# TensorE's loop without a lead-in and with its head placed by `head_slot`, and joined copies of neighbouring ranges, in a float32 transpose of 8192 x 8192

## Chip, cores, metric

One core of one Trainium2 chip. The metric is the device time of a whole execution, in microseconds (us). A transfer has "landed" when the last raise of its semaphore is in the trace; the "granted clock" is the share of TensorE's full clock that the trace records.

## The reference

```python
def setup_inputs():
    return {"x": np.random.randn(8192, 8192).astype(np.float32)}

def reference(x):
    return np.transpose(x)
```

268.44 MB go in and as many come out. Nothing is computed.

## The kernel before

The input is worked through in T = 128 tiles of 128 rows x 4096 columns (two slabs of columns, 64 tiles each). For each tile: a load of 2 MiB into one of three input buffers; 32 transposes of 128 x 128 on TensorE into the eight PSUM banks, four to a bank; eight copies to SBUF, by ScalarE (even banks) and VectorE (odd banks). The copies fill eight "windows" of output, one for each bank, each eight tiles wide; the windows are staggered, so that in each tile one of them is full and is stored (2 MiB as a rule). There are nine window buffers for eight open windows. All loads but the first three and all stores are issued from ScalarE's queue.

```python
        ins = [nc.alloc_sbuf_tensor(f"in{k}", [P, J], dt).ap() for k in range(NIN)]            # NIN = 3
        regs = [nc.alloc_sbuf_tensor(f"reg{k}", [P, B * W * P], dt).ap() for k in range(NREG)]  # NREG = 9
        pss = [nc.alloc_psum_tensor(f"ps{k}", [P, B * P], dt).ap() for k in range(NR)]          # NR = 8
        ...
        def transposes(t):
            k = t % NIN
            nc.tensor.sem_inc(s_ld[k], -16).wait_op(s_ld[k], 16, "sem-ge")
            for q in range(NR):
                if t:
                    nc.tensor.sem_inc(s_bank[q], -1).wait_op(s_bank[q], 1, "sem-ge")
                for b in range(B):                                                              # B = 4
                    tr = nc.tensor.transpose(pss[q][:, b * P:(b + 1) * P],
                        ins[k][:, q * B * P + b:(q + 1) * B * P - B + b + 1:B], ident)
                    if b == B - 1:
                        tr.then_inc(s_pe, 1)
        ...
        for t in range(T % NIN):                        # lead-in: two tiles
            transposes(t)
        with nc.Fori(0, T // NIN, engines=[nc.tensor.engine]):   # 42 turns of three tiles
            for t in range(NIN):
                transposes(T % NIN + t)
        ...
        for t, (s, c) in enumerate(chunks):
            closing = []
            for q in range(NR):
                e = q % 2
                eng = (nc.scalar, nc.vector)[e]
                ...                                     # a new window waits for its buffer's store
                eng.wait_ge(s_pe, t * NR + q + 1)
                ...                                     # one copy of 128 x 512
                before = []
                if e == 0:
                    before, closing = closing, []
                ...                                     # full windows go to closing, the bank is freed
                for k in before:
                    store(*k)
            for k in closing:
                store(*k)
            if t + NIN < T:
                nc.scalar.wait_ge(s_pe, (t + 1) * NR)
                load(t + NIN)
```

## Time and profile before

| | before |
|---|---|
| time, first three runs | 1264.88 us (1264.87 to 1265.91) |
| DMA engines | share 1.01 and 428 GB/s from 2 to 1254 us |
| TensorE (matmul) | busy 744.9 us, 59%; granted clock 0.745 |
| VectorE, ScalarE | busy 348.1 and 294.1 us, 28 and 23% |

The groups of instructions of the kernel before, by line (line, engine, operation, out<-in, forms, count, then busy us, mean ns of one, and idle time before them with what ended it):

```profile
L112 PE MATMUL ps<-ident,in 128*128 128x128 f32 x4096 | 744.9, 364 | 489.8 <-PEq L110 481.4
L189 DVE COPY reg<-ps 128x512 f32<-128x512 f32 x512 | 348.1, 690 | 887.2 <-PE ps L112 733.5
L187 ACT COPY reg<-ps 128x512 f32<-128x512 f32 x512 | 292.9, 588 | 941.5 <-PE ps L112 746.2
```

All three engines are idle for hundreds of us, waiting for each other or for transfers. The busy shares say who is not the bound.

### The profile page before, as it was taken

What the parts mean: (1) busy time and instruction counts of PE and PEld (TensorE: products, weight loads), DVE (VectorE), ACT (ScalarE), POOL (GpSimd) and SP (SyncE); (2) the same over time, 40 slices, a digit from 0 to 9 for tenths busy, and PEclk for the clock granted to TensorE, in tenths of its full rate; (3) what the DMA queues carried; (4) which work ended last, traced back from release to release, by engine and by line L of the source; (5) the groups of instructions that cost most, each with busy time, mean ns of one, the idle gap of its engine ahead of it and who ended that gap; (6) DMA issues with size and microseconds to landing.
All of it is one profiled execution on the core that took longest, in us unless ns stands there. A gap on an engine that the chain in (4) does not pass through costs nothing. (4 is left out here: it accounts for less than half of the span.)

```text
span 1261.5 us, 11043 instructions
## 1 busy us (share of the span) xinstructions
PE 744.9 (59%) x4096; PEld 724.6 (57%) x4096; DVE 348.1 (28%) x512; ACT 294.1 (23%) x513; POOL 0.7 (0%) x6
## 2 busy tenths in 40 slices
PE   5656656565566656565655565656566665656561
PEld 5656656565566656565655555656455655655561
DVE  3322322223222322232222232232222322222220
ACT  3322222222222222222222222222222222222220
POOL 0000000000000000000000000000000000000000
PEclk9877776768677777778687778686867777686765
DMA  9999999999999999999999999999999999999998
GB/s 381 426 427 429 425 430 431 428 429 431 429 429 431 429 429 430 429 430 431 426 428 411 429 429 429 430 431 429 429 431 428 430 430 429 429 429 430 430 429 355
DMA packets 39277, 537.00 MB, mean 426 GB/s; under 512 B 4320, under 2 KB 4832, under 8 KB 6240
## 3 DMA queue, kind: packets, MB, share of 16 engines
q10 hardware_dynamic: 38832, 530.60, 98.9%
q1 hardware_dynamic: 432, 6.29, 1.2%
q14 instruction: 12, 0.10, 0.0%
q8 instruction: 1, 0.02, 0.0%
HBM read 268.44 MB, written 268.44 MB: 426 GB/s over the span
## 5 line engine op out<-in xcount | busy, mean ns | idle before, releaser
L112 PE MATMUL ps<-ident,in 128*128 128x128 f32 x4096 | 744.9, 364 | 489.8 <-PEq L110 481.4
L112 PEld LDWEIGHTS ps<-ident,in 128*128 128x128 f32 x4096 | 724.6, 219 | 509.9 <-issue 509.9
L189 DVE COPY reg<-ps 128x512 f32<-128x512 f32 x512 | 348.1, 690 | 887.2 <-PE ps L112 733.5
L187 ACT COPY reg<-ps 128x512 f32<-128x512 f32 x512 | 292.9, 588 | 941.5 <-PE ps L112 746.2
L187 ACT ACT_TABLE_LOAD x1 | 1.3, 1283 | 0.9 <-SPq L68 0.9
L84 POOL TENSOR_SCALAR_AFFINE_SELECT ident<-ident 128x128 f32<-128x128 f32 x1 | 0.3, 294 | 0.2 <-POOL ident L82 0.2
L82 POOL MEMSET ident<- 128x128 f32 x1 | 0.2, 205 | 0.5 <-SPq L68 0.5
L224 POOL MEMSET const-bfloat16-1.0<- 128x1 bf16 x1 | 0.1, 102 | 0.0
L224 POOL MEMSET const-uint8-127<- 128x1 uint8 x1 | 0.1, 102 | 0.0
L224 POOL MEMSET const-float32-0.0<- 128x1 f32 x1 | 0.1, 99 | 0.2 <-issue 0.2
L224 POOL MEMSET const-float32-1.0<- 128x1 f32 x1 | 0.1, 99 | 0.0
## 6 DMA issues: line engine op xcount, KB each, us to landing
in<-in_x_dram ACTq DMA_DIRECT2D x125, 2048.0 KB, 22.8
out_dram<-reg ACTq DMA_DIRECT2D x114, 2048.0 KB, 19.4
out_dram<-reg ACTq DMA_DIRECT2D x4, 1792.0 KB, 17.6
in<-in_x_dram SPq DMA_DIRECT2D x3, 2048.0 KB, 11.7
out_dram<-reg ACTq DMA_DIRECT2D x4, 1536.0 KB, 15.1
out_dram<-reg ACTq DMA_DIRECT2D x4, 1280.0 KB, 16.3
out_dram<-reg ACTq DMA_DIRECT2D x4, 1024.0 KB, 16.6
out_dram<-reg ACTq DMA_DIRECT2D x4, 768.0 KB, 16.3
```

The costliest lines, as they stand in the source:

```text
L82: nc.gpsimd.memset(ident, 0.0).then_inc(s_id, 1)
L84: nc.gpsimd.affine_select(out=ident, in_=ident, compare_op=mybir.AluOpType.not_equal, fill=1.0, base=0, pattern=[[-1, P]], channel_multipl ...
L112: tr = nc.tensor.transpose(pss[q][:, b * P:(b + 1) * P], ins[k][:, q * B * P + b:(q + 1) * B * P - B + b + 1:B], ident,)
L187: cp = nc.scalar.copy(out=o, in_=i)
L189: cp = nc.vector.tensor_copy(out=o, in_=i)
L224: nc = _bacc.Bacc("TRN2", target_bir_lowering=False, num_devices=1)
```

## The change

Its intent is less work beside the transfers: half as many bank waits on TensorE, 631 copies instead of 1024, and a loop whose head `head_slot=0` puts at a set place in TensorE's program. (The recorded texts call that place a block boundary, and I say "the boundary" below; experiment 2 takes it away.) The eight banks become four double banks, and one copy moves both halves if their two places in SBUF have the same stride. The nine window buffers become one tensor, so that one access pattern can reach two of them.

```diff
-        regs = [nc.alloc_sbuf_tensor(f"reg{k}", [P, B * W * P], dt).ap() for k in range(NREG)]
-        pss = [nc.alloc_psum_tensor(f"ps{k}", [P, B * P], dt).ap() for k in range(NR)]
+        SIZE = B * W * P
+        regs = nc.alloc_sbuf_tensor("regs", [P, NREG * SIZE], dt).ap()
+        pss = [nc.alloc_psum_tensor(f"ps{k}", [P, 2 * B * P], dt).ap() for k in range(NR // 2)]
...
-            for q in range(NR):
-                if t:
-                    nc.tensor.sem_inc(s_bank[q], -1).wait_op(s_bank[q], 1, "sem-ge")
-                for b in range(B):
+            for h in range(NR // 2):
+                nc.tensor.sem_inc(s_bank[h], -1).wait_op(s_bank[h], 1, "sem-ge")
+                for b in range(2 * B):
...
-        for t in range(T % NIN):
-            transposes(t)
-        with nc.Fori(0, T // NIN, engines=[nc.tensor.engine]):
-            for t in range(NIN):
-                transposes(T % NIN + t)
+        for h in range(NR // 2):
+            nc.tensor.sem_inc(s_bank[h], 1)
+        with nc.Fori(0, T // NIN + 1, engines=pe, head_slot={pe[0]: 0}) as turn:
+            with nc.tensor.If(turn > 0):
+                transposes(NIN - 1)
+            nc.tensor.wait_ge(s_id, 2)
+            for k in range(NIN - 1):
+                transposes(k)
...
-            for q in range(NR):
-                e = q % 2
+            for h in range(NR // 2):
+                e = h % 2
...
+                gap = place[1][0] - place[0][0]
+                runs = [(0, 1)]
+                if place[0][1] != place[1][1] or abs(gap) >= 2 ** 15:
+                    runs = [(0,), (1,)]
+                eng.wait_ge(s_pe, t * NR // 2 + h + 1)
...
+                for u in runs:
+                    off, dist = place[u[0]]
+                    dims = [list(regs.ap[0]), [gap, len(u)], [dist, B], [1, P]]
+                    o = bass.AP(regs.tensor, regs.offset + off, dims)
...
+                    cp = nc.scalar.copy(out=o, in_=i) if e == 0 else nc.vector.tensor_copy(out=o, in_=i)
```

The stores and loads, their sizes and their order are untouched.

More of the change, by code (lines that the diff above doesn't have):

```diff
@@ L77 @@
         s_st = [nc.alloc_semaphore(f"s_st{k}") for k in range(NREG)]
-        s_bank = [nc.alloc_semaphore(f"s_bank{q}") for q in range(NR)]
+        s_bank = [nc.alloc_semaphore(f"s_bank{q}") for q in range(NR // 2)]
         s_pe = nc.alloc_semaphore("s_pe")
@@ L100, in load, with transposes @@
             ).then_inc(s_ld[t % NIN], 16)
-        def transposes(t):
-            k = t % NIN
+        def transposes(k):
             nc.tensor.sem_inc(s_ld[k], -16).wait_op(s_ld[k], 16, "sem-ge")
-            for q in range(NR):
-                if t:
-                    nc.tensor.sem_inc(s_bank[q], -1).wait_op(s_bank[q], 1, "sem-ge")
-                for b in range(B):
+            for h in range(NR // 2):
+                nc.tensor.sem_inc(s_bank[h], -1).wait_op(s_bank[h], 1, "sem-ge")
+                for b in range(2 * B):
+                    j = (2 * h + b // B) * B * P + b % B
                     tr = nc.tensor.transpose(
-                        pss[q][:, b * P:(b + 1) * P],
-                        ins[k][:, q * B * P + b:(q + 1) * B * P - B + b + 1:B],
+                        pss[h][:, b * P:(b + 1) * P],
+                        ins[k][:, j:j + B * P - B + 1:B],
                         ident,
                     )
-                    if b == B - 1:
-                        tr.then_inc(s_pe, 1)
+                tr.then_inc(s_pe, 1)
         T = len(chunks)
-        nc.tensor.wait_ge(s_id, 2)
-        for t in range(T % NIN):
-            transposes(t)
-        with nc.Fori(0, T // NIN, engines=[nc.tensor.engine]):
-            for t in range(NIN):
-                transposes(T % NIN + t)
+        assert T % NIN == NIN - 1
+        pe = [nc.tensor.engine]
+        for h in range(NR // 2):
[6 more added lines that the diff above has]
+                transposes(k)
         for t in range(NIN):
@@ L144, in store @@
                 dst = dst.rearrange("(q b) i -> q b i", q=P)
-                src = regs[r][:, base:base + B * rows]
+                src = regs[:, r * SIZE + base:r * SIZE + base + B * rows]
                 base += B * rows
@@ L162 @@
             closing = []
-            for q in range(NR):
-                e = q % 2
+            for h in range(NR // 2):
+                e = h % 2
                 eng = (nc.scalar, nc.vector)[e]
-                if q not in window:
-                    span = (q - c) % W + 1
-                    r = free.pop(0)
-                    parts = [(s, c, min(c + span, CH))]
-                    if c + span > CH and t + span < T:
-                        parts.append((s + 1, 0, c + span - CH))
-                    window[q] = (t, r, parts)
-                    if stored[r]:
-                        eng.wait_ge(s_st[r], 16 * stored[r])
-                t0, r, parts = window[q]
-                k = [p[0] for p in parts].index(s)
-                base = B * P * sum(z - a for _, a, z in parts[:k])
-                _, a, z = parts[k]
-                view = regs[r][:, base:base + B * (z - a) * P].rearrange("p (b i) -> p b i", b=B)
-                o = view[:, :, (c - a) * P:(c - a + 1) * P]
-                i = pss[q].rearrange("p (b i) -> p b i", b=B)
-                eng.wait_ge(s_pe, t * NR + q + 1)
-                if e == 0:
-                    cp = nc.scalar.copy(out=o, in_=i)
-                else:
-                    cp = nc.vector.tensor_copy(out=o, in_=i)
@@ new lines @@
+                place = []
+                for q in (2 * h, 2 * h + 1):
+                    if q not in window:
+                        span = (q - c) % W + 1
+                        r = free.pop(0)
+                        parts = [(s, c, min(c + span, CH))]
+                        if c + span > CH and t + span < T:
+                            parts.append((s + 1, 0, c + span - CH))
+                        window[q] = (t, r, parts)
+                        if stored[r]:
+                            eng.wait_ge(s_st[r], 16 * stored[r])
+                    t0, r, parts = window[q]
+                    k = [p[0] for p in parts].index(s)
+                    base = r * SIZE + B * P * sum(z - a for _, a, z in parts[:k])
+                    _, a, z = parts[k]
+                    place.append((base + (c - a) * P, (z - a) * P))
@@ L190 @@
+                ends = [q for q in (2 * h, 2 * h + 1) if closes(window[q], t)]
+                gap = place[1][0] - place[0][0]
[3 more added lines that the diff above has]
+                eng.wait_ge(s_pe, t * NR // 2 + h + 1)
                 before = []
@@ L192 @@
                     before, closing = closing, []
-                if closes(window[q], t):
-                    cp.then_inc(s_cp[e], 1)
-                    copied[e] += 1
-                    closing.append((q, e, copied[e]))
-                    eng.wait_ge(s_cp[e], copied[e])
-                    eng.sem_inc(s_bank[q], 1)
-                else:
-                    cp.then_inc(s_bank[q], 1)
+                for u in runs:
+                    off, dist = place[u[0]]
+                    dims = [list(regs.ap[0]), [gap, len(u)], [dist, B], [1, P]]
+                    o = bass.AP(regs.tensor, regs.offset + off, dims)
+                    i = pss[h][:, u[0] * B * P:(u[-1] + 1) * B * P]
+                    i = i.rearrange("p (l b i) -> p l b i", b=B, i=P)
+                    cp = nc.scalar.copy(out=o, in_=i) if e == 0 else nc.vector.tensor_copy(out=o, in_=i)
+                    mine = [q for q in ends if q - 2 * h in u]
+                    if mine:
+                        cp.then_inc(s_cp[e], 1)
+                        copied[e] += 1
+                        closing += [(q, e, copied[e]) for q in mine]
+                    if u is runs[-1]:
+                        if mine:
+                            eng.wait_ge(s_cp[e], copied[e])
+                            eng.sem_inc(s_bank[h], 1)
+                        else:
+                            cp.then_inc(s_bank[h], 1)
                 for k in before:
@@ L205 @@
             if t + NIN < T:
-                nc.scalar.wait_ge(s_pe, (t + 1) * NR)
+                nc.scalar.wait_ge(s_pe, (t + 1) * NR // 2)
                 load(t + NIN)
```

## The prediction

> **What bounds the kernel now.** I read the page first, its slices and its DMA part, because a transpose computes nothing: it moves 268.44 MB in and as much out.
>
> ```profile
> PE   5656656565566656565655565656566665656561
> DVE  3322322223222322232222232232222322222220
> ACT  3322222222222222222222222222222222222220
> DMA  9999999999999999999999999999999999999998
> GB/s 381 426 427 429 425 430 431 428 429 431 429 429 431 429 429 430 429 430 431 426 428 411 429 429 429 430 431 429 429 431 428 430 430 429 429 429 430 430 429 355
> HBM read 268.44 MB, written 268.44 MB: 426 GB/s over the span
> ```
>
> TensorE is busy in five to six tenths of every slice, the two copying engines in two to three, and the 16 DMA engines in nine or more of all but the last. The rate is flat at 429 GB/s or so. So the DMA engines are the bound, and everything that the change touches (TensorE's program, the copies) runs beside them.
>
> Next I asked for stretches, to see how much of the span is not at the full rate:
>
> ```profile
> 2.00:1254.00 1252.00, 744.88 (x4096) 724.56 (x4096) 348.15 (x512) 293.04 (x513) 0.00 (x0) 0.75 1.01 428
> 0.00:2.00 2.00, 0.00 (x0) 0.00 (x0) 0.00 (x0) 1.10 (x1) 0.70 (x6) 1.00 0.18 33
> 1254.00:1262.00 8.00, 0.00 (x0) 0.00 (x0) 0.00 (x0) 0.00 (x0) 0.00 (x0) 0.50 0.34 143
> ```
>
> The last two columns are the DMA share and the GB/s. For 1252 us the share is 1.01 at 428 GB/s. Only the first 2 us and the last 8 us are below, and they moved 33 x 2 us = 0.07 MB and 143 x 8 us = 1.14 MB, which at 428 GB/s would have taken 2.8 us. So at most 10 - 2.8 = 7.2 us of 1261.5, 0.6%, are not at the DMA's rate[...]. No change to the compute engines can take more than this away.
>
> The chain that ended last is no guide here: it names 1% of work, the last tile's, since a queued DMA is not a step of it. The waits tell who waits for whom:
>
> ```profile
> ACT reg L187 <- PE ps L112: 746.2, 384, 7.3
> DVE reg L189 <- PE ps L112: 733.5, 400, 10.4
> PE ps L112 <- PEq L110: 481.4, 125, 5.1
> ACT reg L187 <- DMA out_dram<-reg: 192.5, 45, 9.1
> DVE reg L189 <- DMA out_dram<-reg: 153.3, 39, 8.3
> ```
>
> The 125 waits of TensorE are one per tile (128 tiles). They are put down to the bank wait of L110, but the timeline shows the 32 transposes of one tile back to back (6.06 to 6.44 us when the granted clock is low) and then an idle stretch of about 3.5 us until the next tile. So I take the real releaser to be the load of the tile, which the DMA delivers every 1253 / 128 = 9.8 us. TensorE has about 3.5 us to spare in each.
>
> Last, how far ahead the transfers are issued:
>
> ```profile
> in<-in_x_dram ACTq DMA_DIRECT2D x125, 2048.0 KB, 22.8
> out_dram<-reg ACTq DMA_DIRECT2D x114, 2048.0 KB, 19.4
> ```
>
> A 2 MiB transfer takes 2.097 / 428 = 4.9 us of all engines. A load lands 22.8 us after its issue, a store 19.4. This adds up: three input buffers turn over in 3 x 9.8 = 29.4 us, and 22.8 of queue plus the 6.4 us that TensorE reads is 29.2. So at each issue about three other transfers, 14.7 us of work, lie ahead in the queue. An issue that comes 1 to 3 us later shortens this queue and nothing else.
>
> [...] The trace does not show the loop paying for it now: its compare-and-branch took 208 ns, the next matmul followed at once, and the fetch queue moved 12 packets, 0.10 MB[...]. [...]
>
> **The change, part by part.** The instruction order of both kernels shows that all 266 transfers of ScalarE's queue are the same, in the same sequence; the three first loads too. Bytes, descriptor sizes and order do not change. This is the main reason for the number.
>
> 1. Copies. ScalarE: 512 become 192 joined and 128 single (where the two places have different strides). VectorE: 201 joined and 110 single. [...] ScalarE's busy time: 128 x 0.588 + 192 x 1.015 = 270 us, from 293. VectorE's: 110 x 0.69 + 201 x 1.223 = 322 us, from 348. Some 25 us less on each, all of it beside the DMA: 0 us on the path.
>
> 2. Semaphores of TensorE. 8 bank waits per tile become 4: 1016 waits of 51 ns become 512, about 26 us of sequencer time, 0.2 us a tile, inside the 3.5 us of idle time. 0 us.
>
> 3. The loop. One lead-in of two tiles goes; a conditional part and one more turn come: 43 turns with a second branch of about 0.2 us, 9 us in all, in the same idle time. At the start TensorE waits until 8.4 us for its first load, so an extra fetch there is hidden. 0 us.
>
> 4. What becomes later. A copy now waits for eight transposes instead of four, 0.5 to 0.85 us, and takes 0.4 to 0.5 us longer, so stores are issued 1 to 2 us later; loads not, as they wait for the whole tile. In the middle the 14.7 us of queue absorbs it. I therefore expect the store's time from issue to landing to fall from 19.4 to about 18, and the landing itself to stay.
>
> 5. The tail is the one place without a queue to hide in. No loads follow there. The last load landed at about 1228.2 us; behind it lay two stores[...]. Before, the first of the eight last stores was issued at 1231.8. After, it comes behind both copies of the third pair: the sixth group of transposes is done at 1233.6, two single copies take 1.2 us, so it is issued at 1234.9, 3.1 us later, and its data begin about 1 us after, at 1236. That is just in time; I put 0 to 2 us on it, 0.5 in the middle.
>
> Sum: 1264.9 + 0.5, less a few tenths if something at the start gains: 1265.2 us.
>
> **Rivals.** A: the gain intended. If fetches or copies were on the path, 25 us of copies and 26 us of waits would come off, 2% each. Against it: the DMA share of 1.01 for 1252 us. Only the 7.2 us of the ends are open, so even in the best case about 1258 us. B: the coarser hand-over starves the DMA. Twice as large a unit in PSUM means four places instead of eight, and one copy that waits for a store to free its place now holds up two groups. The waits for stores (84 times, 346 us) speak for it. Against it: when such a store lands, three transfers are still queued, and what must follow (two copies of 1.0 us and an issue of 0.6 us) takes 3 us of those 14.7. If I am wrong and 1 us were lost in each tile, the time would be 1390 us; 0.2 us a tile makes 1290. C: the branch at every turn, or the conditional part, makes TensorE wait for a fetch. [...] but a turn has 3 x 3.5 us to spare; the time stays 1265. D: the tail empties the queue by more than I allow: 1267 to 1268.
>
> **Range and chances.** The three timed runs lie within 1.04 us. Nothing in the stretch of 1252 us should move; the ends can move by about -2 to +3 us. Eight times in ten: 1262.5 to 1268. Faster by over 2% would need less than 1239.6 us, below the 1254 us in which the bytes pass at 428 GB/s: 0.5%. Slower by over 2% needs 0.2 us of starvation in every tile or a surprise in the new branches: 1.5%.
>
> **What would show it.** Right: DMA share at 1.01 in the middle and the slices at 428 to 431 GB/s; VectorE near 322 us and ScalarE near 270 in 311 and 320 copies; a joined copy near 1.02 and 1.22 us; the store's time to landing shorter, at 18 us or so; the last stores first issued at about 1235, perhaps with a dip in the DMA share around 1236. Wrong: slices in the middle under 425 GB/s, or TensorE waits longer than the 3.5 to 5 us of now with DMA share under 1, would mean B or C. A span shorter by more than 7 us would mean that the DMA rate is not the limit I take it for.

The forecast was 1264.9 + 0.5 us, less a few tenths, 1265.2 us; parts 1 to 4 stood in it as 0 us each, the tail as 0.5, and terms from which parts 1 and 5 were worked out are among the cuts. What they leave open:

- That no rate was left to win was not shown; the slices of the kernel before read 425 to 431 GB/s in the middle but for one of 411.
- In "paying for it", "it" is a fetch of instructions at each turn. The "fetch queue" is the profile's instruction queue q14, with its 12 packets in 42 turns.
- The 1.015 and 1.223 us of a joined copy, and the 270 and 322 us made of them, were my estimates. The page of the changed kernel has 1013 and 1224 ns, which is 425 and 534 ns more than the 588 and 690 ns of a single copy before, and 262.9 and 316.0 us.
- "Just in time" speaks of the moment at which the queue was to run dry, put at about 1236 us with an allowance that no trace shows. In the kernel before, the last packet ended at 1259.80 us and the last landing came at 1260.20, 0.4 us later. The 1 us from an issue to its data is in that trace: the first load was issued at 0.94 us and its first packet of 16 KiB began at 1.94.

## The result

The changed kernel took 1265.55 us (median of six runs, 1263.88 to 1266.72), the kernel before 1265.35 us in the same comparison (six runs, 1264.87 to 1265.91). The ratio is 1.0001, 95% interval 0.9988 to 1.0014. Ratios here are the mean time of one kernel's runs over that of the other's of the same rounds, so not quite the ratio of the medians that I quote. Differences under about 1.6 us (0.0013 of the time, the half width of the interval) are not resolved. The outputs are right.

The slices and the DMA part of the page of the changed kernel:

```profile
PE   5665565565556555665556655656556655656561
DVE  2322222222222222223222222222222222222220
ACT  2312121122212211222212121122212121122120
DMA  9999999999999999999999999999999999999998
GB/s 367 430 426 426 426 428 430 429 431 430 429 428 430 430 430 428 430 429 429 430 421 420 428 429 427 427 426 428 427 431 429 431 429 429 429 430 429 430 429 364
```

And the stretch from 2 to 1254 us (the last three columns: granted clock, DMA share, GB/s):

```profile
2.00:1254.00 1252.00, 747.47 (x4096) 726.98 (x4096) 316.03 (x311) 261.83 (x321) 0.00 (x0) 0.75 1.01 427
```

The rate is the same 426 to 431 GB/s as before in all but a few slices: the first, the last, and two (421 and 420; before, one of 411) in the middle, where one slab of columns ends and stores are cut in two. The groups of copies, with forms kept apart, and the DMA issues (count, KB each, median us from issue to landing):

```profile
L208 DVE COPY regs<-ps 128x1024 f32<-128x1024 f32 x201 | 245.4, 1224 | 700.5 <-PE ps L114 537.4 <-DMA out_dram<-regs 161.9
L208 ACT COPY regs<-ps 128x1024 f32<-128x1024 f32 x192 | 193.5, 1013 | 746.7 <-PE ps L114 519.2 <-DMA out_dram<-regs 225.8 <-ACT regs L208 0.5
L208 DVE COPY regs<-ps 128x512 f32<-128x512 f32 x110 | 70.8, 686 | 221.3 <-PE ps L114 170.2 <-DMA out_dram<-regs 50.8
L208 ACT COPY regs<-ps 128x512 f32<-128x512 f32 x128 | 68.7, 589 | 225.7 <-PE ps L114 174.4 <-DMA out_dram<-regs 51.0
```

```profile
in<-in_x_dram ACTq DMA_DIRECT2D x125, 2048.0 KB, 22.5
out_dram<-regs ACTq DMA_DIRECT2D x114, 2048.0 KB, 18.3
```

The engines do less, as intended: VectorE 316.0 us and ScalarE 262.9 us, 32 and 31 us under before. The stores reach the queue later and keep their place among the loads: they land 18.3 us after issue instead of 19.4. (In this one profile loads and stores alike land about 1.4 us later than before; experiments 2 and 4 come back to that.) The last stores, in the timeline of the changed kernel and in stretches of 2 us (the last two columns are the DMA share and GB/s):

```profile
1236.36 15.47 ACTq L28 DMA_DIRECT2D out_dram<-regs  x8
```

```profile
1234.00:1236.00 2.00, 2.00 (x12) 2.00 (x11) 0.75 (x2) 0.83 (x2) 0.00 (x0) 0.55 0.85 360
1236.00:1238.00 2.00, 0.42 (x4) 0.23 (x2) 1.29 (x2) 0.24 (x1) 0.00 (x0) 1.00 0.45 187
1238.00:1240.00 2.00, 0.00 (x0) 0.00 (x0) 0.00 (x0) 0.00 (x0) 0.00 (x0) 0.81 1.10 454
```

Here is the predicted dip: a share of 0.45 for 2 us, 1.1 us of all engines. Before, the same stretch reads:

```profile
1236.00:1238.00 2.00, 0.00 (x0) 0.00 (x0) 0.00 (x0) 0.50 (x1) 0.00 (x0) 0.79 1.01 427
```

And one thing that I had not foreseen: the first matmul. Timelines of the start, before and then after:

```profile
8.40 9.34 PE L112 MATMUL ps<-ident,in 128*128 128x128 f32 x64 [8.40 <-PEq L107]
```

```profile
9.92 9.61 PE L114 MATMUL ps<-ident,in 128*128 128x128 f32 x64 [9.92 <-PEq L111]
```

TensorE starts 1.5 us later. So two small losses are to be seen, 1.5 us at the start and 1.1 us at the end, and neither shows in the time. The experiments are about where they went.

**A reading that the page does not give.** Each load's semaphore is raised 16 times, and the trace has the time of each. I call each raise the landing of a share, and take it for that of one of the 16 DMA engines; this is my reading and was not shown, as the trace does not name the engine. "The slowest engine" below is a name for the last of the 16 raises. What the trace does show is how far the 16 shares are apart, by rank. In the kernel before, all 16 shares of the first load landed within 0.46 us of each other (7.80 to 8.26 us). From about 150 us on the last came 3.5 us behind the first, from the change of slab on (690 us) 4.6 us, and at the last load 5.0 us. By rank the distances stay the same for hundreds of us (3.50 us from first to last at loads 20, 60 and 64), so it seems that some engines are late once and stay late. The last share keeps a pace of 9.76 us a tile in the first slab (9.80 in the second), 4.194 MB / 9.76 us = 430 GB/s.

### The profile page after: what moved, and what is told of

Same layout as the page of the kernel before. It is cut to its first block, busy times and chain, and to the rows that moved or that the text cites. A ratio compares the mean times of both kernels' runs of the same rounds, so it can differ in the third digit from the quotient of the medians.

```text
span 1263.0 us, 10220 instructions
## 1 busy us (share of the span) xinstructions
PE 747.5 (59%) x4096; PEld 727.0 (58%) x4096; DVE 316.0 (25%) x311; ACT 262.9 (21%) x321; POOL 0.7 (0%) x6
## 5 line engine op out<-in xcount | busy, mean ns | idle before, releaser
L208 DVE COPY regs<-ps 128x1024 f32<-128x1024 f32 (+1 forms) x311 | 316.0, 1034 | 921.8 <-PE ps L114 707.6
L208 ACT COPY regs<-ps 128x1024 f32<-128x1024 f32 (+1 forms) x320 | 261.6, 843 | 972.4 <-PE ps L114 693.6
## 6 DMA issues: line engine op xcount, KB each, us to landing
out_dram<-regs ACTq DMA_DIRECT2D x114, 2048.0 KB, 18.3
```

The source lines that it names most:

```text
L208: cp = nc.scalar.copy(out=o, in_=i) if e == 0 else nc.vector.tensor_copy(out=o, in_=i)
```

## The experiments

**1. The parts alone.** Do two effects cancel?

```diff
 loop_only: the kernel before, eight banks and its copies, with
+        with nc.Fori(0, T // NIN + 1, engines=pe, head_slot={pe[0]: 0}) as turn:
+            with nc.tensor.If(turn > 0):
+                transposes(NIN - 1)
 copies_only: the changed kernel with the old lead-in and loop
+        for t in range(T % NIN):
+            transposes(t % NIN)
+        with nc.Fori(0, T // NIN, engines=[nc.tensor.engine]):
+            for t in range(NIN):
+                transposes((T % NIN + t) % NIN)
```

> The kernel before with the new loop alone (conditional part, 43 turns, loop head on a block boundary), 8 banks and 512+512 copies as before. My theory (the DMA engines are the bound, TensorE has 3.5 us to spare per tile): ratio 1.000 +- 0.001, about 1265 us, DMA share 1.01 from 2 to 1254 us. Rival, two effects that cancel: if the loop costs and the copies gain, this run is slower by at least 0.5% (1271 us or more) and the copies alone faster by as much.

> The changed kernel with the old loop (lead-in of two tiles, 42 turns), joined copies and four double banks. My theory: ratio 1.000 +- 0.001; first of the eight last stores issued late (1235 us or after) and a dip of the DMA share at 1236 to 1238 us as in the changed kernel. Rival, two effects that cancel: faster by 0.5% or more (1259 us or less).

Measured: the loop alone 1264.71 us (six runs), ratio 1.0008 (0.9991 to 1.0024); the copies alone 1264.97 us (five runs), ratio 0.9998 (0.9985 to 1.0011). Nothing cancels: each part is worth nothing by itself. The copies alone show the dip (share 0.35 from 1234 to 1236 us) and the loop alone does not (0.98 to 1.02 there), so the dip comes with the copies.

**2. The changed kernel again, and the boundary taken away.** Where does the late first matmul come from?

```diff
 after_again: no edit
 no_head_slot:
-        with nc.Fori(0, T // NIN + 1, engines=pe, head_slot={pe[0]: 0}) as turn:
+        with nc.Fori(0, T // NIN + 1, engines=pe) as turn:
```

> The changed kernel once more, for the spread and for the first load, which landed 1.5 us later than in the kernel before (first matmul at 9.9 instead of 8.4 us). If that is chance of the run: within 0.5 us of either value here and in the other runs, without relation to the loop. If it comes from the new loop (a fetch at the start): 9.9 us here, in the loop alone and with the early tail, and 8.4 us with the copies alone. Ratio 1.000 +- 0.0015.

> The changed kernel without the block boundary for the loop's head. In all four runs with the new loop one of the 16 DMA engines landed its part of the first load at 9.6 to 9.7 us, the other 15 at 7.7 to 8.2; in the two with the old loop all 16 by 8.3 us. If the boundary (the jump to it) is what that engine is busy with: all 16 by 8.3 us here, first matmul at 8.4 us. If the rest of the new loop (conditional part): still one at 9.6 us. The time is 1265 +- 2 us either way, since the lateness was made up by the twentieth tile.

Measured: again 1265.03 us, ratio 0.9997 (0.9984 to 1.0010), first matmul at 9.97 us. In all six profiles with the new loop on its boundary and all tiles as they are, one of the 16 shares of the first load landed at 9.5 to 9.7 us and the other 15 by 8.3 us; before and in the copies alone all 16 landed by 8.3 us. Without the boundary (one look, 1264.36 us) all 16 landed by 8.34 us and the first matmul came at 8.63 us. So the boundary it is. The trace shows what may have held the late share up: each kernel has one packet of 16,384 bytes in an instruction queue, of 0.93 to 0.94 us. It comes at 6.0 us where the loop is on the boundary, at 24.1 and 28.1 us in the kernel before and the copies alone, and at 118.3 us without the boundary. The trace does not name a packet's engine, so this was not shown, but the landings fit it where the packet comes later: in the kernel before (24.1 us), the copies alone (28.1) and the kernel before with eight buffers (25.6, experiment 6) one share of the next load to land was 1.8, 1.3 and 1.3 us behind the other 15, and of the load before that at most 0.2. What is left of the loss by tile 20 (counted from 0) does not go with the boundary: the last share of that load landed at 180.9 us before, 181.5 in the copies alone and 180.8 without the boundary; with it at 180.8 and 180.9 us in the early tail and the repeated run, 180.9 and 181.9 in the two late tails of experiment 4, and 181.7 and 182.3 us in the loop alone and the first run of the changed kernel.

**3. The last stores earlier.**

```diff
 tail_early, in the last tile only, ahead of ScalarE's wait for the third pair:
+                if t == T - 1:
+                    for k in before:
+                        store(*k)
+                    before = []
                 eng.wait_ge(s_pe, t * NR // 2 + h + 1)
```

> The changed kernel, but in the last tile alone the stores of the first two pairs are issued before ScalarE waits for the third pair. If the dip at 1236 to 1238 us (share 0.45, so 1.1 us of all engines) comes from the late issue: first last store at about 1233 us, no 2 us stretch between 1232 and 1250 us under a share of 0.8, and the time 0 to 1.1 us shorter (ratio to before 0.999 to 1.000; this may drown in the spread of the runs). If the dip has another cause (small packets, the landing of the store before), it stays.

Measured: 1265.01 us, ratio 1.0000 (0.9987 to 1.0013). The first last store was issued at 1232.80 us, and the stretch from 1236 to 1238 us is full (share 1.03). But another dip stands at 1232 to 1234 us (share 0.66): the expectation that no stretch would be under 0.8 failed. And the end did not move. This is where my account of the tail fell: the dip goes or stays and the time does not care.

The landings suggest a theory, which no trace shows engine by engine: the end is set by the slowest of the 16 engines alone, and in a dip of the mean share the others are idle while it still has work. If so, the time from the slowest engine's landing of the last load to the last landing of all should be a constant, whatever the dip, until the slowest engine itself runs dry.

**4. The last stores later.** This new theory was put to the test with idle copies on ScalarE ahead of the eight last stores.

```diff
 tail_wait_short: n = 5; tail_wait_long: n = 20
+                if t == T - 1 and h == 2:
+                    delay(n)      # n copies of 128 x 128, and a wait for the last
                 for k in before:
                     store(*k)
```

> The changed kernel, with five idle copies on ScalarE (estimate 0.3 us each, 1.5 us) ahead of the eight last stores. New theory: the end is set by the slowest of the 16 DMA engines alone, which runs 3 to 6 us behind the first; in six runs the last landing came 32.24 to 32.47 us after the slowest engine's part of the last load had landed, with or without the dip. That engine has work until about 9.8 us after that landing less 0.4 us, so it would run dry at about 1238.8 us, and the changed kernel's first last store (issued at 1236.4, data from 1237.4) leaves it 1.4 us. So here: the dip grows to about 2.5 us of all engines, and the interval stays within 32.2 to 32.8 us. Rival (my prediction's step 5: each us of the dip is a us of the end): 33.7 us or more.

> The same with twenty idle copies (estimate 6 us). Now the slowest engine runs dry too: 6 - 1.4 = 4.6 us later than in the changed kernel, interval 36 to 38 us, time 1269 to 1271 us, ratio 1.0035. Rival (step 5): 38.2 us or more. If it stays at 32 us, the issue of the last stores does not matter at all and the theory of the slowest engine is wrong.

Measured: 1264.50 us, ratio 0.9994 (0.9977 to 1.0010), and 1266.57 us, ratio 1.0007 (0.9990 to 1.0024). The copies were quicker than I had estimated, 5 in 1.10 and 20 in 4.09 us. (One by itself reads 298 ns in the mean on the page of experiment 7, but in a row they overlap.) All the profiles with the full transfers and unchanged tiles, by the delay of the first last store:

| kernel | first last store issued, after the slowest landing of the last load, us | end, after that landing, us |
|---|---|---|
| tail_early | 3.5 | 32.25 |
| before | 3.8 | 32.25 |
| loop_only | 3.8 | 32.25 |
| after_again | 5.8 | 32.47 |
| copies_only | 5.9 | 32.25 |
| no_head_slot | 6.8 | 32.24 |
| after | 6.9 | 32.24 |
| tail_wait_short | 6.9 | 32.64 |
| tail_wait_long | 10.2 | 34.49 |

"End" is the last landing of any share. Up to 6.9 us the issue costs nothing, or a few tenths (0.2 and 0.4 us in two profiles, which the theory does not explain). At 10.2 us it costs 2.2 us; if each us past the edge costs one, the edge lies at about 8.0 us, and the changed kernel stands some 1 us short of it. Issued 3.3 us later than in the changed kernel, the rival (a us for a us) would give 32.2 + 3.3 = 35.5, the slowest engine with its 1.4 us to spare 34.1; it was 34.49. So the theory holds within some tenths, in the one profile that goes past the edge; the numbers for the long wait (36 to 38 us, ratio 1.0035) assumed a longer delay and missed, and the 34.1 was worked out afterwards, from the delay measured. The short wait told little: its tile happened to be transposed faster, so that its stores came no later than the changed kernel's.

The line of the long wait in stretches of 2 us, where the share nearly reaches zero:

```profile
1238.00:1240.00 2.00, 0.00 (x0) 0.00 (x0) 0.00 (x0) 2.00 (x11) 0.00 (x0) 1.00 0.10 41
```

What differs between runs is when the slowest engine gets to the last load: 1228.0 us before, 1229.5 in the changed kernel, 1228.3 in the same kernel again, 1229.3 in the copies alone and 1228.1 in the loop alone. That is the spread of the runs, and it goes neither with the loop nor with the copies.

**5. A quarter of the bytes.** Is the DMA truly the bound, and what is the change worth where it is not? Both kernels: a quarter of the columns of each load, one of four rows of each store's block. Their outputs are wrong, which doesn't matter for the times.

```diff
-                out=ins[t % NIN], in_=x[c * P:(c + 1) * P, s * J:(s + 1) * J]
+                out=ins[t % NIN][:, :J // 4], in_=x[c * P:(c + 1) * P, s * J:s * J + J // 4]
...
-                dst = dst.rearrange("(q b) i -> q b i", q=P)
+                dst = dst.rearrange("(q b) i -> q b i", q=P)[:, 0:1, :]
```

> Wrong result on purpose: the kernel before with a quarter of the bytes of each load and store (a quarter of the columns loaded, one of four rows of each block stored); TensorE and the copies do all their work. If the DMA engines were the bound: the DMA needs 537/4 = 134 MB, 313 us at 429 GB/s, and TensorE becomes the bound, at 0.12 us a transpose (4 in 0.48 us at full clock) 32 x 0.12 = 3.84 us a tile, 492 us, with waits 500 to 560 us. If the bound was elsewhere (copies, semaphores, latency), it stays over 1000 us.

> Wrong result on purpose: the changed kernel with the same quarter of the bytes. My theory: with the DMA out of the way this shows what the change is worth on the engines: up to 4 waits of 51 ns a tile, 26 us, less 43 branches of 0.2 us, 9 us, so 0 to 4% under the quarter of the kernel before if TensorE is the bound and its waits are on the path. Rival (coarser hand-over): 2% or more over it, with TensorE waiting for banks.

Measured: 517.80 us for the kernel before, ratio 0.4088 to the full kernel, and 519.64 us for the changed one, ratio 0.4105. The pages' first lines and TensorE's group, one after the other:

```profile
PE 498.1 (97%) x4096; PEld 497.9 (97%) x4096; DVE 354.3 (69%) x512; ACT 296.2 (57%) x513; POOL 8.5 (2%) x9
L114 PE MATMUL ps<-ident,in 128*128 128x128 f32 x4096 | 498.1, 285 | 9.6 <-PEq L109 9.6
```

```profile
PE 498.0 (96%) x4096; PEld 497.5 (96%) x4096; DVE 317.1 (61%) x311; ACT 262.6 (51%) x321; POOL 8.5 (2%) x9
L116 PE MATMUL ps<-ident,in 128*128 128x128 f32 x4096 | 498.0, 285 | 9.7 <-PEq L113 9.7
```

With the transfers cut, the time falls by 59%, so they are the bound. (The run does not tell the 16 engines from the memory and the paths that they use; a quarter of the bytes relieves all of these.) TensorE is now busy 97% of the span and idle only before its first tile and after its last; its granted clock is 0.996 instead of 0.745. And the change still gains nothing: my 0 to 4% were wrong. The waits and branches that it takes away or adds never made the array idle, 498.1 and 498.0 us. What is left, 0.4%, is hardly more than the noise (the intervals of the two ratios, 0.4079 to 0.4098 and 0.4092 to 0.4118, overlap) and is most likely the late last stores, with no queue to hide them: the first was issued at 505.96 us before and at 508.02 us after.

**6. The slack of the stores taken away.** Eight window buffers instead of nine, so that a store must land before the next tile can reuse its place.

```diff
-    NREG = 9
+    NREG = 8
```

> The kernel before with 8 store buffers instead of 9, so that a store must land before the next tile's copies into its place: this takes the slack of the stores away. Estimate: each store is then issued only after the one before has landed, with about one load in the queue; 0 to 3 us lost a tile, 1265 to 1650 us. It gives the base for the next run.

> The changed kernel with 8 store buffers. My theory: the 1 to 2 us by which the joined copies delay each store are hidden only by the queue; with the queue taken away they show, so this run is slower than the kernel before with 8 buffers, by 0.5 to 2 us a tile (60 to 250 us). If the two are equal within 1%, the coarser hand-over costs nothing even without the queue, and my reading of what absorbs it is wrong.

Measured: 1331.20 us, ratio 1.0518 (1.0488 to 1.0549), and 1351.37 us, ratio 1.0673 (1.0648 to 1.0699). The direction is as expected: without the spare buffer the changed kernel takes 20 us more. That this is the coarser hand-over and not the loop is argued; no run with eight buffers has the one without the other. The size is not as expected: 20 / 128 = 0.16 us a tile, not 0.5 to 2. The issues of 2 MiB stores, before and after with eight buffers:

```profile
out_dram<-reg ACTq DMA_DIRECT2D x114, 2048.0 KB, 10.6
```

```profile
out_dram<-regs ACTq DMA_DIRECT2D x114, 2048.0 KB, 9.1
```

If the landings kept their place, the joined copies make a store 1.5 us later here too (10.6 less 9.1), and only a tenth of that reaches the time. The stretches of these two runs carry a warning:

```profile
2.00:1254.00 1252.00, 712.79 (x3940) 673.14 (x3940) 315.11 (x488) 270.05 (x494) 0.00 (x0) 0.75 1.00 406
```

```profile
2.00:1254.00 1252.00, 701.41 (x3896) 663.51 (x3896) 294.78 (x270) 245.09 (x269) 0.00 (x0) 0.75 1.00 400
```

The DMA share still reads 1.00 at 406 and 400 GB/s. The packets of 16 KiB took 647 and 655 ns in the mean instead of 615, at the same median of 611: some packets took longer, and their longer time counts as busy. So the share alone does not prove that the DMA moves all that it can; the rate has to be read beside it, 406 and 400 GB/s here against 428 with nine buffers.

**7. Every store later.** The doubled cost: idle copies ahead of each tile's store, in the changed kernel.

```diff
 mid_delay:
+                if h == 2 and t < T - 1:
+                    delay(14)
                 for k in before:
                     store(*k)
```

> The changed kernel with fourteen idle copies on ScalarE (estimate 4 us) ahead of the store in every tile but the last, two to four times the 1 to 2 us by which the joined copies delay it. Theory of the queue: the store's time to landing falls from 18.3 by about the delay, to 14 to 15 us, the load's from 22.5 to 19 or so, and the time stays within 1264 to 1267 us (ratio within 0.002 of 1). Rival (coarser hand-over costs): if a tenth of the delay reached the DMA, 128 x 0.4 = 51 us more, ratio 1.04.

Measured: 1276.45, 1325.26, 1337.29 and 1339.31 us. Three of the four count as slow, being over 1.5% above the fastest, though their granted clock (0.735 to 0.744) is near the fast one's 0.749. The delay was 2.89 us a tile (14 copies). Even the fast run is 0.9% above the kernel before, 11 us, where I expected 0.2% at most and the queue should have hidden all of it. That is 0.09 us a tile of the 2.89, in a single run. The one profile is of a slow run; its slices and its two issues of 2 MiB:

```profile
GB/s 335 416 431 429 427 431 431 430 429 427 430 430 421 430 425 425 426 421 416 422 420 414 410 408 395 393 363 385 383 373 380 376 376 362 386 388 374 364 333 348
in<-in_x_dram ACTq DMA_DIRECT2D x125, 2048.0 KB, 20.2
out_dram<-regs ACTq DMA_DIRECT2D x114, 2048.0 KB, 16.2
```

The rate is whole for the first third and then sinks. The landings show 15 shares within about 0.5 us of each other from the ninetieth tile on, and one that is 10 to 12 us behind them; the 15 keep its pace, 11.1 us a tile. As I count a store or load as landed only when its last share has, a queue of 20 us is for the other 15 one of 20 - 11 = 9 us. So I would take the lag of the slowest engine off the slack that I counted on, 14.7 us; this is argued, from a run that counts as slow, and no run shows it. Why the lag grows here and not in the other kernels, and why that last share itself falls from 9.8 to 11.1 us a tile, stays open: the trace does not tell which packet ran on which engine. As three of these runs are slow ones, nothing is explained by them; from the fast one I take only that 3 us more a tile are not hidden wholly.

## Why the prediction was right, point by point

- **The bound.** Right, and shown by the quarter of the bytes (517.8 us) and by the rate, 430 GB/s at the pace of the last share (428 in the stretch from 2 to 1254 us). That I took the share of 1.01 as a proof was right by luck: it reads 1.00 at 400 GB/s too.
- **Transfers unchanged.** Right: the same packets of 16 KiB and smaller, the same rate in the slices. ScalarE's queue has 267 transfers, not 266, and both traces have them in one order with the same shapes. This carried the number. The sign of being wrong, "slices in the middle under 425 GB/s", was set too sharply: the changed kernel has 421 and 420, but the kernel before has 411 there.
- **Copies (part 1).** A joined copy took 1013 and 1224 ns; the estimates were 1015 and 1223. ScalarE's busy time was 262.9 us instead of 270, VectorE's 316.0 instead of 322, because two single copies in a row overlap: two took 1.07 and 1.29 us, not 2 x 0.588 and 2 x 0.690. On the path: 0, as predicted.
- **Waits and loop (parts 2 and 3).** 0 us, as predicted, and no gain even where TensorE is the bound. One small reading was off: the second branch took 77 ns in the median, not 0.2 us (the one that ends a turn took 208 ns in the median, in both kernels). One sentence failed: "an extra fetch there is hidden". With the boundary one of the 16 shares of the first load landed 1.4 us late and TensorE began 1.5 us late. It cost nothing that the time shows: without the boundary 1264.36 us (one run), with it 1265.03 and 1265.55 us, in the spread of the runs.
- **Later stores (part 4).** Right: 18.3 us to landing, predicted about 18.
- **The tail (part 5).** The mechanism was seen as predicted: the first store 6.9 us after the last load's slowest landing (predicted 1234.9 - 1228.2 = 6.7), and a dip at 1236 us. The mis-sized term is its cost, put at 0.5 us. Within the few tenths by which like profiles differ, it is 0.0 us: 32.24 us from that landing to the end against 32.25 before. I had treated the 16 engines as one queue that runs dry at once. The 16 shares of the last load landed 3.4 to 6.4 us apart (3.4 in the changed kernel); by my reading of the landings only the slowest engine counts, and that one did not run dry.
- **Rival A** was rightly turned down. **Rival B** was turned down with an allowance that is probably too large: later stores can cost time (20 us with one buffer less; 11 us in the fast run with 3 us more of delay), though the change as it is loses nothing by them. **Rivals C and D** did not come: the instruction queues moved 11 packets in the 43 turns of the changed kernel (13 in the 42 turns before), so not one at each turn, and the tail cost nothing.

The predicted 1265.2 us and the measured 1265.55 us differ by less than the spread of the runs, so the 0.5 us of the tail could not have been told from the time; the landings told it.

## What to carry to other kernels

When transfers bound the kernel, ask first whether a change alters the bytes, the packets or the order of the transfers. Here it did not; what it took off the other engines was worth nothing, and what it made later was free only as far as the queue reached. Before calling a delay hidden, count that queue for the slowest of the 16 engines and subtract its lag (argued, not shown). A dip in the mean DMA share need not be a loss: here a dip to 0.45 cost nothing (32.24 us from the last load's last share to the end, 32.25 without it), and the one to 0.10 cost 2.2 us; by my reading the slowest engine had run dry too. And a share of 1.00 is no proof of the full rate: it read 1.00 at 400 GB/s with eight buffers and 1.01 at 428 with nine.
